# An encoder block in split float32 on one core: both seeds of the seven-product scheme made late, from copies that ScalarE takes of a chain sum

## The chip, the cores and the metric

The kernel runs on one core of a Trainium2 chip. The metric is the device time of one execution in microseconds (us), lower is better. PE is TensorE, DVE is VectorE, ACT is ScalarE, POOL is GpSimd, SP issues most loads.

## The reference

One layer of a hybrid encoder for 256 rows of width 2048, float32 throughout:

```python
h = rms_norm(x, g_mix); proj = h @ w_in          # q, k, v of three attention branches, and 3 gates
oa, ob, oc = ...                                 # dilated windows; grouped-query; cross-attention to mem
gates = sigmoid(gt).reshape(b, s, 3, 2048)
merged = gates[0]*(oa @ w_br_a) + gates[1]*(ob @ w_br_b) + gates[2]*(oc @ w_br_c)
x = x + merged @ w_o
hf = rms_norm(x, g_ffn) @ w_ffn_in               # 2048 -> 2 x 5632
x = x + (silu(hf[..., :5632]) * hf[..., 5632:]) @ w_ffn_out
```

The change touches what comes from the gates on: the gate and branch products with their merge, the output projection, and the FFN.

## The kernel before

**Split products.** Every float32 factor is kept as a high part and a remainder, and each product of blocks is three matmuls: high by high, high by low, low by high. For a weight block (raw, 128 x 1024) ACT makes the high part (`whi`, L413) and DVE the remainder (`wlo`, L423). The activations (xT, oT, mT, x1T, hT) lie ready in both parts. There are five rotating buffers each for whi and wlo, so whi of a step can't be made before PE has ended the step five places earlier.

**Pairs.** From 310 us on the work is a row of 24 pairs: five for the gates (`merging`, blocks b = 0, 1, 2, the last two with two pairs each, j = 0 and 2), two for the output projection (O and O2, `projecting`), eleven for the FFN's input and six for its output (`feeding`). A pair makes two output blocks of 256 x 512 at once, in four accumulators, the PSUM banks X, Y, W and Q. Some of the contraction is done with seven products where eight are usual, on sums of weight blocks and of activations (`forms`). One double m has the seven steps X, W, P, Y, Q, Z, H, each of six matmuls of 128x512. P and Q need a weight sum or difference that DVE makes first (L537, L539), and so does H (L541). The rest of the contraction is done by whole blocks: d into X and Y, D into W and Q.

**Banks and seeds.** P, Q and H accumulate in bank X on top of X's products, one behind the other, so X holds a chain sum; Z accumulates in bank W. At the end of X's products ACT copies bank X to bank Y (L514) as Y's start. At the end of W's, ACT copies bank W to SBUF as m5 (L517; the profile writes m). At the end of P's, DVE writes m5 − X into bank W (L519), and at the end of Q's, m5 − X into bank Q (L523). These two are the seeds of the last two output blocks. Where a bank is fresh, PE sets it with one dummy matmul first (`wake`).

**Order.** A step list per stage, written by hand, sets the order of the steps: l and r are loads (l also starts the POOL queue's accumulating load of the sum of two blocks), a letter with a number is a step, and a point takes one step of the tail that the pair before has left. The second string of a list is worked off without tails, and the third becomes the tail. `run(..., 4)` readies each step (load, weight sum, whi, wlo) four steps ahead of its matmuls; the instructions of each engine then stand in that program order and run in it. `done` functions empty the banks: `gates` and `merge` (L838, L843, L849), `add` (L883), `hidden` (L924 with the Silu table, L927), `output` (L946). Jobs such as the transposes run beside the steps; a `yield n` in one lets n steps pass.

In `add`, the fourth block's job squares its rows, lets two steps pass, transposes, lets two more pass, and then makes the reciprocal root (`row_scale`, L140 to L157: eleven small DVE operations and two copies to the scales), which the Silu of the first FFN pair needs.

Of the kernel before, what the change touches and what calls it, by code (L numbers as in the profile page):

```python
# [11 lines left out]
F32 = mybir.dt.float32  # L12
# [38 lines left out]

STEPS_GATE = ("l0 l1 X0 . X1 . . r0 W0 r1 W1 P0 P1 . Y0 Y1 . Q0 Q1 .", "Z0 Z1 D4 H0 D5 H1 d4 D6 d5 D7 d6 d7", "")
STEPS_O = ("l0 X0 . . r0 . W0 . P0 . Y0 . Q0", "Z0 D2 H0 D3 d2 D6 D7 D4 D5", "d3 d6 d7 d4 d5")
STEPS_O2 = ("l0 X0 . r0 W0 . P0 . Y0 . Q0 .", "Z0 D2 H0 D3 d2 D4 D5 d3 D6 D7", "d4 d5 d6 d7")
STEPS_FFN0 = ("l0 l1 X0 X1 . r0 W0 . r1 W1 . P0 P1 . Y0 Y1 Q0 Q1", "Z0 Z1 D6 H0 D7 H1 D4 D5", "d6 d7 d4 d5")
STEPS_FFN = ("l0 l1 X0 X1 . r0 W0 r1 W1 P0 P1 . Y0 Y1 . Q0 Q1 .", "Z0 Z1 D4 H0 D5 H1 D6 D7", "d4 d5 d6 d7")
STEPS_OUT = STEPS_OUT2 = STEPS_FFN
STEPS_LAST = ("l0 l1 X0 X1 . r0 W0 . r1 W1 . P0 P1 . Y0 Y1 Q0 Q1", "Z0 Z1 H0 H1 D4 D5", "d4 d5")  # L60
# [41 lines left out]
def encoder_block(ctx: ExitStack, tc: tile.TileContext, a: dict, out: bass.AP):  # L102
# [17 lines left out]
    def s4(shape, name, dt=F32):  # L120
        return mid.tile(shape, dt, name=name, tag="s4")
# [300 lines left out]
        while len(due) > n:  # L422
            nc.follow(nc.vector.tensor_sub(*due.pop(0)))  # L423

    def pair(src, lhs, lists, done, doubles=(), forms=None, operand=None, fresh=False):

# [71 lines left out]

        def wake(b, hi):

            if fresh:
                nc.tensor.matmul(ps[b], lhsT=hi[:, 0, :P], rhs=hi[:, 0], start=True, stop=True)

        def phase_end(kind, hi):
            seen[kind] = seen.get(kind, 0) + 1
            if seen[kind] < nd:
                return
            with tc.high_priority():  # L510
                if kind == "X":
                    new("Y")
                    wake("Y", hi)
                    nc.follow(nc.scalar.activation(ps["Y"], ps["X"], AF.Copy))  # L514
                elif kind == "W":
                    raws["m5"] = s4([P, NC], "m5")
                    nc.follow(nc.scalar.activation(raws["m5"], ps["W"], AF.Copy))  # L517
                elif kind == "P":
                    nc.follow(nc.vector.tensor_sub(ps["W"], raws["m5"], ps["X"]))  # L519
                elif kind == "Q":  # L520
                    new("Q")
                    wake("Q", hi)
                    nc.follow(nc.vector.tensor_sub(ps["Q"], raws["m5"], ps["X"]))  # L523

        def seventh(kind, m):
            of = {"X": "b11", "W": "t", "Y": "b21", "P": "t", "Z": "b22", "Q": "b11", "H": "b21"}[kind]
            bk = {"P": "X", "Q": "X", "H": "X", "Z": "W"}.get(kind, kind)
            needs = {"Y": "X", "P": "X", "Z": "P", "Q": "P", "H": "Q"}

            def ready():  # L530
                r = raws[m]
                raw = r[of]
                if kind in "PQH" and last_kind[0] == {"P": "W", "Q": "X", "H": "Y"}[kind] + str(m):
                    low(0)
                last_kind[0] = kind + str(m)
                if kind == "P":
                    nc.follow(nc.vector.tensor_add(raw, raw, r["b22"]))  # L537
                elif kind == "Q":
                    nc.follow(nc.vector.tensor_sub(raw, r["t"], raw))  # L539
                elif kind == "H":  # L540
                    nc.follow(nc.vector.tensor_add(raw, r["t"], raw))  # L541
                hi, lo = halves(raw)
                for n in {"Q": ["b11"], "Z": ["b22"], "H": ["t", "b21"]}.get(kind, ()):
                    release(r.pop(n))

                def products():
                    assert kind not in needs or seen.get(needs[kind], 0) == nd, (kind, seen)
                    assert kind != "Z" or seen["W"] == nd
# [281 lines left out]
    def merging():  # L830
        for b, (g0, k0, k1) in enumerate(((0, 0, 2), (8, 2, 6), (4, 6, 12))):
            for j in (0, 2) if b else (2,):
                sg = [None, None]

                def gates(c, r, sg=sg):
                    sg[c] = s4([P, T, NC], "sg")
                    for t in range(T):
                        nc.scalar.activation(sg[c][:, t], r[t], AF.Sigmoid, scale=r_x[:, 0, t:t + 1])  # L838

                def merge(c, r, j=j, b=b, sg=sg):  # L840
                    n0 = (j + c) * NC
                    for t in range(T):
                        nc.vector.tensor_mul(sg[c][:, t] if b else mg[t][:, n0:n0 + NC], r[t], sg[c][:, t])  # L843

                    def later():
                        yield 1
                        for t in range(T):
                            m = mg[t][:, n0:n0 + NC]
                            nc.vector.tensor_add(m, m, sg[c][:, t])  # L849
                        if b == 2:  # L850
                            to = mT[j + c] = s8([P, 2, 4, S], "mT", pool=home(j + c))
                            if j + c == 0:
                                room.extend(form_room(1))
                            yield 3
                            yield from transposed([mg[t][:, n0:n0 + NC] for t in range(T)],
                                                  lambda k, n: (to[:, 0, k:k + n], to[:, 1, k:k + n]),
                                                  lag=2, also=room[0] if j + c == 0 else None)
                    if b:
                        start(urgent(later()))

                yield pair(block_pair(a["w_gate"], g0 + j), xT, STEPS_GATE, gates, TWO, by_room(lambda: gforms),
                           fresh=b == 0)
# [6 lines left out]
    def projecting():  # L869
# [9 lines left out]
        for n in (0, 2):  # L879
            def add(c, r, n=n):  # L880
# [6 lines left out]
                def later():  # L887
                    yield 1
                    sq = s4([P, T, NC], "sq")
                    for t in range(T):  # L890
                        nc.scalar.activation(sq[:, t], xc[t], AF.Square, accum_out=ss1[:, t, n + c:n + c + 1])
                    yield 2
                    if not x1T:
                        x1T.extend(s8([P, 2, 4, S], "x1T") for _ in range(4))
                        room.extend(form_room(3))
                    yield from transposed(xc, lambda k, m: (x1T[n + c][:, 0, k], x1T[n + c][:, 1, k]),
                                          lambda k: gT[:, 2, 4 * (n + c) + k:4 * (n + c) + k + 1], 2,
                                          also=room[2 + n + c] if n == 0 else None)
# [13 lines left out]
    def feeding():  # L912
        for c0, c1 in ((0, 4), (4, 8), (8, KF // 4)):
# [3 lines left out]
            for n in range(c0, c1):  # L917
                av = []

                def hidden(c, v, av=av, n=n - c0, hT=hT):  # L920
# [8 lines left out]
                    def later():  # L929
# [115 lines left out]
```

## Time and profile before

| | us |
|---|---|
| median of 3 runs (lowest, highest) | 1374.86 (1374.70, 1375.64) |
| the profiled execution's own time | 1373.56 |
| its span | 1371.8 |
| PE busy | 1355.9 (99%) |
| DVE busy | 1154.8 (84%) |
| ACT busy | 852.1 (62%) |

The granted clock of TensorE is 0.999 over the span. The stages: up to 310 us the projections and attention, gates to 600 (with the O pair's start), output projection to about 690, FFN to the end. PE's busy share says little here, since its rows overlap; how far it stands still is read from the gaps between a matmul and the next, and from what released the next. In rows of the timeline, start, duration, engine, line, operation and out<-in are followed by the idle time before, with its releaser, in square brackets. The profile leaves out buffer numbers, so mmX is bank X of any pair and raw any weight block.

### The profile page before, as it was taken

Reading aid. Unit: us, or ns where it says so; the run is one execution under the profiler, and the core shown is the slowest. Engines: PE = TensorE matmul, PEld = TensorE weight load, DVE = VectorE, ACT = ScalarE, POOL = GpSimd, SP = SyncE. Lnnn points to the kernel's source line nnn. Section 1 sums busy time; section 2 is a strip of 40 time slices with the busy share of each in tenths; the row PEclk is TensorE's granted clock in tenths of the full one; section 3 lists DMA queues with packets and bytes.
Section 4 is the critical chain, followed back from the end, with each engine's and each line's share of the span. In section 5 each row is a group of like instructions: output and inputs, shape, how many; then the busy total and the mean of one; then the engine's idle time right before and its main releaser. Section 6 shows DMA issues by size and latency. Waiting matters only on the chain.

```text
span 1371.8 us, 17290 instructions
## 1 busy us (share of the span) xinstructions
PE 1355.9 (99%) x6170; PEld 1121.2 (82%) x6170; DVE 1154.8 (84%) x1411; ACT 852.1 (62%) x1101; POOL 53.2 (4%) x60
## 2 busy tenths in 40 slices
PE   9999999999999999999999999999999999999998
PEld 8878888887787878788878888888888888888887
DVE  6878877779779779778888998888999889989997
ACT  7776666656555555657666666655666655566664
POOL 0010000000000000000000000000000000000000
PEclk9999999999999999999999999999999999999999
DMA  9976455566595595865577666786666786666873
GB/s 368 344 233 212 140 153 182 155 176 223 173 313 172 184 307 156 290 229 166 172 245 227 189 227 203 250 264 215 212 217 218 250 269 191 221 224 214 278 211 108
DMA packets 86342, 301.18 MB, mean 220 GB/s; under 512 B 9776, under 2 KB 12336, under 8 KB 86000
## 3 DMA queue, kind: packets, MB, share of 16 engines
q1 hardware_dynamic: 79488, 275.94, 57.8%
q0 software_dynamic: 6624, 24.12, 9.3%
q8 instruction: 48, 0.79, 0.2%
q14 instruction: 38, 0.31, 0.1%
q10 hardware_dynamic: 144, 0.02, 0.0%
HBM read 297.17 MB, written 2.88 MB: 219 GB/s over the span
## 4 chain that ended last, share of the span: by engine, by line
PE 93%; DVE 5%; issue 1%; ACT 1%; POOL 0%; DVEq 0%; ACTq 0%; POOLq 0%
PE mmX L77 28%; PE mmW L77 19%; PE mm L77 16%; PE mmY L77 14%; PE mmQ L77 11%; DVE wlo L423 3%; PE tp L77 1%; PE sc L77 1%; PE o L77 1%; PE pT L77 1%; DVE raw L539 1%; PE hT L77 0%; DVE sg L843 0%; ACT whi L413 0%; PE idle L77 0%
## 5 line engine op out<-in xcount | busy, mean ns | idle before, releaser
L413 ACT ACTIVATE whi<-raw 128x1024 fp32r<-128x1024 f32 (+1 forms) x359 | 372.2, 1054 | 227.8 <-PE mmQ L77 49.4
L423 DVE TENSOR_TENSOR wlo<-raw,whi 128x1024 fp32r<-128x1024 f32 (+1 forms) x359 | 432.4, 1217 | 94.5 <-ACT whi L413 91.4
L77 PE MATMUL mm<-whi,xT 128*128 128x512 f32 x640 | 202.8, 393 | 0.1
L413 ACT ACTIVATE whi<-more 128x1024 fp32r<-128x1024 f32 x102 | 107.7, 1056 | 68.1 <-DVE more L539 17.5
L131 DVE TENSOR_TENSOR wlo<-raw,whi 128x1024 fp32r<-128x1024 f32 x82 | 103.0, 1258 | 44.8 <-ACT whi L130 43.8
L423 DVE TENSOR_TENSOR wlo<-more,whi 128x1024 fp32r<-128x1024 f32 x102 | 124.2, 1220 | 18.8 <-ACT whi L413 17.8
L77 PEld LDWEIGHTS mm<-whi,xT 128*128 128x128 f32 x640 | 119.5, 188 | 24.2 <-DVE V L134 0.5
L413 ACT ACTIVATE whi<-both 128x1024 fp32r<-128x1024 f32 x92 | 97.2, 1057 | 66.0 <-issue 12.1
L130 ACT ACTIVATE whi<-raw 128x1024 fp32r<-128x1024 f32 x82 | 86.8, 1060 | 66.7 <-PE mm L77 52.1
L423 DVE TENSOR_TENSOR wlo<-both,whi 128x1024 fp32r<-128x1024 f32 x92 | 112.0, 1221 | 19.3 <-ACT whi L413 18.5
L77 PE MATMUL mmW<-whi,forms 128*128 128x512 f32 x368 | 123.2, 394 | 4.1 <-ACT av L924 3.3
L77 PE MATMUL mm<-wlo,xT 128*128 128x512 f32 x320 | 125.8, 393 | 0.0
L77 PE MATMUL mmX<-whi,forms 128*128 128x512 f32 x368 | 122.0, 391 | 2.3 <-DVE mmW L519 2.3
L77 PE MATMUL mmX<-whi,x1T 128*128 128x512 f32 x352 | 120.9, 389 | 0.0
L77 PE MATMUL mmY<-whi,x1T 128*128 128x512 f32 x264 | 88.9, 389 | 0.0
L77 PEld LDWEIGHTS mmW<-whi,forms 128*128 128x128 f32 x368 | 69.7, 190 | 19.8 <-ACT av L924 3.7
L77 PEld LDWEIGHTS mmX<-whi,forms 128*128 128x128 f32 x368 | 69.1, 188 | 17.3 <-ACT whi L413 3.1
L77 PEld LDWEIGHTS mmX<-whi,x1T 128*128 128x128 f32 x352 | 66.1, 188 | 13.7
L77 PE MATMUL mmW<-wlo,forms 128*128 128x512 f32 x184 | 72.3, 393 | 0.0
L77 PE MATMUL mmX<-wlo,forms 128*128 128x512 f32 x184 | 71.7, 390 | 0.0
L77 PEld LDWEIGHTS mm<-wlo,xT 128*128 128x128 f32 x320 | 60.2, 188 | 12.2 <-issue 0.7
L77 PE MATMUL mmX<-wlo,x1T 128*128 128x512 f32 x176 | 68.5, 389 | 0.0
(269 smaller groups left out, 2588.9 us busy)
## 6 DMA issues: line engine op xcount, KB each, us to landing
raw<-in_w_ffn SPq DMA_DIRECT2D x110, 512.0 KB, 6.5
raw<-in_w_gate SPq DMA_DIRECT2D x68, 512.0 KB, 4.7
raw<-in_w_qkv SPq DMA_DIRECT2D x64, 512.0 KB, 4.2
raw<-in_w_ffn_out SPq DMA_DIRECT2D x55, 512.0 KB, 6.8
more<-in_w_ffn SPq DMA_DIRECT2D x33, 512.0 KB, 7.5
both<-in_w_ffn SPq DMA_DIRECT2D x33, 512.0 KB, 5.8
raw<-in_w_o SPq DMA_DIRECT2D x22, 512.0 KB, 5.8
more<-in_w_ffn_out SPq DMA_DIRECT2D x20, 512.0 KB, 5.0
```

The costliest lines, as they stand in the source:

```text
L77: ins = op(*args, **kw)
L130: nc.scalar.activation(hi, src, AF.Copy)
L131: nc.vector.tensor_sub(lo, src, hi.bitcast(F32))
L413: nc.follow(nc.scalar.activation(hi[:, o], v, AF.Copy))
L423: nc.follow(nc.vector.tensor_sub(*due.pop(0)))
L539: nc.follow(nc.vector.tensor_sub(raw, r["t"], raw))
```

## The change

The m5 copy goes. At the end of P's products, and again at the end of Q's, ACT copies the chain sum in bank X to SBUF (u, L520 after). When Q's has been copied, DVE makes both seeds from bank W and these copies: Q = W − u of Q, then W = W − u of P (L525, two rows). Thus Z needs Q's end and not P's, and H needs no more than the copy. The step lists are rewritten for this, those of the gates one per stage: H goes ahead of Z and D, and in some lists Y1 stands behind Q1. `fresh` now names the banks that get the dummy matmul: Y and Q for block 0, Y for the first pair of block 1 (before: Y and Q for block 0). One call per tag shifts the banks by one place ahead of the gates. In `add`, `row_scale` moves ahead of the transposes, one step behind the squares.

```diff
-STEPS_GATE = ("l0 l1 X0 . X1 . . r0 W0 r1 W1 P0 P1 . Y0 Y1 . Q0 Q1 .", "Z0 Z1 D4 H0 D5 H1 d4 D6 d5 D7 d6 d7", "")
+STEPS_GATE = {
+    0: ("l0 l1 X0 X1 r0 W0 r1 W1 P0 P1 Y0 Q0 Q1 Y1 H0 H1", "Z0 D4 Z1 D5 d4 D6 d5 D7 d6 d7", ""),
+    1: ("l0 l1 X0 . X1 r0 W0 r1 W1 P0 P1 . Y0 Q0 Q1 Y1 H0 H1", "Z0 D4 Z1 D5 d4 D6 d5 D7 d6 d7", ""),
+    2: ("l0 l1 X0 . . X1 r0 W0 r1 W1 P0 P1 . Y0 Y1 Q0 Q1 . H0 H1", "Z0 D4 Z1 D5 d4 D6 d5 D7 d6 d7", ""),
+    3: ("l0 l1 X0 . . . X1 r0 W0 r1 W1 . P0 P1 . Y0 Y1 Q0 Q1 . H0 H1", "Z0 D4 Z1 D5 d4 D6 d5 D7 d6 d7", "")}
-STEPS_O = ("l0 X0 . . r0 . W0 . P0 . Y0 . Q0", "Z0 D2 H0 D3 d2 D6 D7 D4 D5", "d3 d6 d7 d4 d5")
+STEPS_O = (". . . l0 X0 . r0 W0 . P0 . Q0 Y0", "H0 d2 Z0 D2 D3 D6 D7 D4 D5", "d3 d6 d7 d4 d5")
-STEPS_FFN0 = ("l0 l1 X0 X1 . r0 W0 . r1 W1 . P0 P1 . Y0 Y1 Q0 Q1", "Z0 Z1 D6 H0 D7 H1 D4 D5", "d6 d7 d4 d5")
-STEPS_FFN = ("l0 l1 X0 X1 . r0 W0 r1 W1 P0 P1 . Y0 Y1 . Q0 Q1 .", "Z0 Z1 D4 H0 D5 H1 D6 D7", "d4 d5 d6 d7")
+STEPS_FFN0 = ("l0 l1 X0 X1 . r0 W0 . r1 W1 . P0 P1 . Y0 Q0 Q1 Y1 H0 H1", "Z0 D6 Z1 D7 D4 D5", "d6 d7 d4 d5")
+STEPS_FFN = ("l0 l1 X0 X1 . r0 W0 r1 W1 P0 P1 . Y0 Y1 Q0 Q1 . H0 H1 .", "Z0 D4 Z1 D5 D6 D7", "d4 d5 d6 d7")
-STEPS_LAST2 = ("l0 l1 X0 X1 . r0 W0 r1 W1 P0 P1 . Y0 Y1 Q0 Q1", "Z0 Z1 D4 H0 D5 H1 d4 d5", "")
+STEPS_LAST2 = ("l0 l1 X0 X1 . r0 W0 r1 W1 P0 P1 . Y0 Q0 Q1 Y1 H0 H1", "Z0 D4 Z1 D5 d4 d5", "")
...
-                elif kind == "W":
-                    raws["m5"] = s4([P, NC], "m5")
-                    nc.follow(nc.scalar.activation(raws["m5"], ps["W"], AF.Copy))
-                elif kind == "P":
-                    nc.follow(nc.vector.tensor_sub(ps["W"], raws["m5"], ps["X"]))
-                elif kind == "Q":
+                elif kind in "PQ":
+                    raws[kind] = s4([P, NC], "u")
+                    nc.follow(nc.scalar.activation(raws[kind], ps["X"], AF.Copy))
+                if kind == "Q":
                     new("Q")
                     wake("Q", hi)
-                    nc.follow(nc.vector.tensor_sub(ps["Q"], raws["m5"], ps["X"]))
+                    for to, u in (("Q", "Q"), ("W", "P")):
+                        nc.follow(nc.vector.tensor_sub(ps[to], ps["W"], raws[u]))
...
-            needs = {"Y": "X", "P": "X", "Z": "P", "Q": "P", "H": "Q"}
+            needs = {"Y": "X", "P": "X", "Z": "Q", "Q": "P", "H": "Q"}
...
+    for tag in ("tp", "c1"):
+        bank("first", tag)
...
-                yield pair(block_pair(a["w_gate"], g0 + j), xT, STEPS_GATE, gates, TWO, by_room(lambda: gforms),
-                           fresh=b == 0)
+                yield pair(block_pair(a["w_gate"], g0 + j), xT, STEPS_GATE[b + (j // 2 if b else 0)], gates, TWO, by_room(lambda: gforms),
+                           fresh=("YQ", "Y" if j == 0 else "", "")[b])
...
+                    if last:
+                        yield 1
+                        ssr = small.tile([P, T], F32, name="ss", bufs=1)
+                        nc.vector.tensor_reduce(ssr, ss1, axis=AX.X, op=ALU.add)
+                        row_scale(ssr, r_f)
                     yield 2
...
-                    if last:
-                        yield 2
-                        ssr = small.tile([P, T], F32, name="ss", bufs=1)
-                        nc.vector.tensor_reduce(ssr, ss1, axis=AX.X, op=ALU.add)
-                        row_scale(ssr, r_f)
...
-            pairs = (STEPS_LAST, STEPS_LAST2) if last else (STEPS_OUT, STEPS_OUT2)
+            pairs = (STEPS_LAST, STEPS_LAST2) if last else (STEPS_FFN, STEPS_FFN)
```

O2's and the first of the last two pairs' lists change in the same manner. Lines after the change are numbered three higher from L77 on and a little more further down: whi is L416, wlo L426, Q's weight differences L541, H's L543.

How the instructions stand, at three places. First gate pair 1 (block 0), the rows of ACT from Y0's copy on before the change: Y0, Y1, m5, Q0, Q1, then Z0, Z1 and D4, and only then H0.

```order
L413 ACTIVATE whi<-raw_3346 128x1024
L413 ACTIVATE whi<-more_3354 128x1024
L517 ACTIVATE m_3407<-mmW 128x512
L413 ACTIVATE whi<-raw_3329 128x1024
L413 ACTIVATE whi<-raw_3334 128x1024
L413 ACTIVATE whi<-raw_3344 128x1024
L413 ACTIVATE whi<-raw_3352 128x1024
L413 ACTIVATE whi<-more_3452 128x1024
L413 ACTIVATE whi<-raw_3346 128x1024
```

The same stretch of ACT after: Y0, Q0, Q1, Y1, u of P, H0, H1, Z0, u of Q, D4.

```order
L416 ACTIVATE whi<-raw_3348 128x1024
L416 ACTIVATE whi<-raw_3331 128x1024
L416 ACTIVATE whi<-raw_3336 128x1024
L416 ACTIVATE whi<-more_3356 128x1024
L520 ACTIVATE u<-mmX 128x512
L416 ACTIVATE whi<-raw_3348 128x1024
L416 ACTIVATE whi<-more_3356 128x1024
L416 ACTIVATE whi<-raw_3346 128x1024
L520 ACTIVATE u<-mmX 128x512
L416 ACTIVATE whi<-more_3471 128x1024
```

H0 has moved up by three places, H1 directly behind it, and the copy that both seeds need stands behind them and Z0. DVE in the same pair before, from Y0's wlo to the seed of Q (L539 makes Q's weights, L541 H's):

```order
L423 TENSOR_TENSOR wlo<-raw_3346,whi 128x1024
L539 TENSOR_TENSOR raw_3329<-raw_3327,raw_3329 128x1024
L423 TENSOR_TENSOR wlo<-more_3354,whi 128x1024
L539 TENSOR_TENSOR raw_3334<-raw_3332,raw_3334 128x1024
L423 TENSOR_TENSOR wlo<-raw_3329,whi 128x1024
L519 TENSOR_TENSOR mmW<-m_3407,mmX 128x512
L423 TENSOR_TENSOR wlo<-raw_3334,whi 128x1024
L423 TENSOR_TENSOR wlo<-raw_3344,whi 128x1024
L423 TENSOR_TENSOR wlo<-raw_3352,whi 128x1024
L541 TENSOR_TENSOR raw_3346<-raw_3327,raw_3346 128x1024
L423 TENSOR_TENSOR wlo<-more_3452,whi 128x1024
L523 TENSOR_TENSOR mmQ<-m_3407,mmX 128x512
```

DVE after, from the row behind P1's wlo to both seeds (L541 makes Q's weights, L543 H's):

```order
L541 TENSOR_TENSOR raw_3331<-raw_3329,raw_3331 128x1024
L426 TENSOR_TENSOR wlo<-raw_3348,whi 128x1024
L541 TENSOR_TENSOR raw_3336<-raw_3334,raw_3336 128x1024
L426 TENSOR_TENSOR wlo<-raw_3331,whi 128x1024
L426 TENSOR_TENSOR wlo<-raw_3336,whi 128x1024
L543 TENSOR_TENSOR raw_3348<-raw_3329,raw_3348 128x1024
L426 TENSOR_TENSOR wlo<-more_3356,whi 128x1024
L543 TENSOR_TENSOR more_3356<-raw_3334,more_3356 128x1024
L426 TENSOR_TENSOR wlo<-raw_3348,whi 128x1024
L426 TENSOR_TENSOR wlo<-more_3356,whi 128x1024
L525 TENSOR_TENSOR mmQ<-mmW,u 128x512
L525 TENSOR_TENSOR mmW<-mmW,u 128x512
```

H's two additions have moved ahead of Y1's wlo and of Z's, and both seeds stand together behind H1's wlo.

Second, ACT at the second FFN pair before: whi of a tail step, of W0, W1, P0, the start of Y, whi of P1 and of a tail step, then the load of the Silu table and the Silu itself (av).

```order
L413 ACTIVATE whi<-raw_6442 128x1024
L413 ACTIVATE whi<-raw_6407 128x1024
L413 ACTIVATE whi<-raw_6411 128x1024
L413 ACTIVATE whi<-raw_6407 128x1024
L514 ACTIVATE mmY<-mmX 128x512
L413 ACTIVATE whi<-raw_6411 128x1024
L413 ACTIVATE whi<-raw_6527 128x1024
L924 ACT_TABLE_LOAD
L924 ACTIVATE av<-mmW,scales 128x512
L924 ACTIVATE av<-mmQ,scales 128x512
```

After, with the same names of steps:

```order
L416 ACTIVATE whi<-raw_6462 128x1024
L416 ACTIVATE whi<-raw_6427 128x1024
L928 ACT_TABLE_LOAD
L928 ACTIVATE av<-mmW,scales 128x512
L928 ACTIVATE av<-mmQ,scales 128x512
L416 ACTIVATE whi<-raw_6432 128x1024
L416 ACTIVATE whi<-raw_6427 128x1024
L517 ACTIVATE mmY<-mmX 128x512
L416 ACTIVATE whi<-raw_6432 128x1024
```

The table load and the Silu stand directly behind W0's whi, ahead of five instructions that stood before them; they follow the scales, whose last row on DVE is now ahead of W0's wlo.

Third, DVE in the last pair before, from Y0's wlo to H's first addition (L946 adds the pair before into x):

```order
L423 TENSOR_TENSOR wlo<-raw_11430,whi 128x1024
L539 TENSOR_TENSOR raw_11383<-raw_11381,raw_11383 128x1024
L423 TENSOR_TENSOR wlo<-more_11452,whi 128x1024
L519 TENSOR_TENSOR mmW<-m_11518,mmX 128x512
L539 TENSOR_TENSOR more_11387<-both,more_11387 128x1024
L946 SCALAR_TENSOR_TENSOR x_5534<-mmY,scales,x_5534 128x512
L423 TENSOR_TENSOR wlo<-raw_11383,whi 128x1024
L946 SCALAR_TENSOR_TENSOR x_5554<-mmX,scales,x_5554 128x512
L423 TENSOR_TENSOR wlo<-more_11387,whi 128x1024
L423 TENSOR_TENSOR wlo<-raw_11428,whi 128x1024
L423 TENSOR_TENSOR wlo<-raw_11450,whi 128x1024
L541 TENSOR_TENSOR raw_11430<-raw_11381,raw_11430 128x1024
```

After, from the row behind the tail step's wlo to H's second addition (L950 adds into x):

```order
L541 TENSOR_TENSOR raw_11434<-raw_11432,raw_11434 128x1024
L426 TENSOR_TENSOR wlo<-more_11482,whi 128x1024
L541 TENSOR_TENSOR raw_11439<-raw_11437,raw_11439 128x1024
L426 TENSOR_TENSOR wlo<-raw_11434,whi 128x1024
L950 SCALAR_TENSOR_TENSOR x_5550<-mmY,scales,x_5550 128x512
L950 SCALAR_TENSOR_TENSOR x_5570<-mmX,scales,x_5570 128x512
L426 TENSOR_TENSOR wlo<-raw_11439,whi 128x1024
L543 TENSOR_TENSOR more_11482<-raw_11432,more_11482 128x1024
L426 TENSOR_TENSOR wlo<-both,whi 128x1024
L543 TENSOR_TENSOR both<-raw_11437,both 128x1024
```

H's additions have moved ahead of Z's remainders, and both of the old seed's subtractions have left this stretch.

More of the change, by code (lines that the diff above doesn't have):

```diff
@@ L48 @@
 MEM_SLOTS = [("kc", _i) for _i in range(4)] + [("vc", _i) for _i in range(4)]
-STEPS_GATE = ("l0 l1 X0 . X1 . . r0 W0 r1 W1 P0 P1 . Y0 Y1 . Q0 Q1 .", "Z0 Z1 D4 H0 D5 H1 d4 D6 d5 D7 d6 d7", "")
-STEPS_O = ("l0 X0 . . r0 . W0 . P0 . Y0 . Q0", "Z0 D2 H0 D3 d2 D6 D7 D4 D5", "d3 d6 d7 d4 d5")
-STEPS_O2 = ("l0 X0 . r0 W0 . P0 . Y0 . Q0 .", "Z0 D2 H0 D3 d2 D4 D5 d3 D6 D7", "d4 d5 d6 d7")
-STEPS_FFN0 = ("l0 l1 X0 X1 . r0 W0 . r1 W1 . P0 P1 . Y0 Y1 Q0 Q1", "Z0 Z1 D6 H0 D7 H1 D4 D5", "d6 d7 d4 d5")
-STEPS_FFN = ("l0 l1 X0 X1 . r0 W0 r1 W1 P0 P1 . Y0 Y1 . Q0 Q1 .", "Z0 Z1 D4 H0 D5 H1 D6 D7", "d4 d5 d6 d7")
-STEPS_OUT = STEPS_OUT2 = STEPS_FFN
-STEPS_LAST = ("l0 l1 X0 X1 . r0 W0 . r1 W1 . P0 P1 . Y0 Y1 Q0 Q1", "Z0 Z1 H0 H1 D4 D5", "d4 d5")
-STEPS_LAST2 = ("l0 l1 X0 X1 . r0 W0 r1 W1 P0 P1 . Y0 Y1 Q0 Q1", "Z0 Z1 D4 H0 D5 H1 d4 d5", "")
+STEPS_GATE = {
[4 rows of a table added]
+STEPS_O = (". . . l0 X0 . r0 W0 . P0 . Q0 Y0", "H0 d2 Z0 D2 D3 D6 D7 D4 D5", "d3 d6 d7 d4 d5")
+STEPS_O2 = ("l0 X0 . r0 W0 . P0 . Q0 . Y0 .", "H0 Z0 D2 D3 d2 D4 D5 d3 D6 D7", "d4 d5 d6 d7")
+STEPS_FFN0 = ("l0 l1 X0 X1 . r0 W0 . r1 W1 . P0 P1 . Y0 Q0 Q1 Y1 H0 H1", "Z0 D6 Z1 D7 D4 D5", "d6 d7 d4 d5")
+STEPS_FFN = ("l0 l1 X0 X1 . r0 W0 r1 W1 P0 P1 . Y0 Y1 Q0 Q1 . H0 H1 .", "Z0 D4 Z1 D5 D6 D7", "d4 d5 d6 d7")
+STEPS_LAST = ("l0 l1 X0 X1 . r0 W0 . r1 W1 . P0 P1 . Y0 Q0 Q1 Y1 H0 H1", "Z0 Z1 D4 D5", "d4 d5")
+STEPS_LAST2 = ("l0 l1 X0 X1 . r0 W0 r1 W1 P0 P1 . Y0 Q0 Q1 Y1 H0 H1", "Z0 D4 Z1 D5 d4 d5", "")
 class InOrder:
@@ L423, in low, with pair @@
             nc.follow(nc.vector.tensor_sub(*due.pop(0)))
-    def pair(src, lhs, lists, done, doubles=(), forms=None, operand=None, fresh=False):
+    def pair(src, lhs, lists, done, doubles=(), forms=None, operand=None, fresh=""):
         lists = [l.split() for l in lists]
@@ L501, in wake @@
         def wake(b, hi):
-            if fresh:
+            if b in fresh:
                 nc.tensor.matmul(ps[b], lhsT=hi[:, 0, :P], rhs=hi[:, 0], start=True, stop=True)
@@ L547, in products @@
                     assert kind not in needs or seen.get(needs[kind], 0) == nd, (kind, seen)
-                    assert kind != "Z" or seen["W"] == nd
+                    assert kind != "Q" or seen["W"] == nd
                     for i in range(2):
```

## The prediction

> **What bounds the kernel now.** I read the page first: the span, the share of each engine, and the chain that ended last.
>
> ```profile
> span 1371.8 us, 17290 instructions
> PE 1355.9 (99%) x6170; PEld 1121.2 (82%) x6170; DVE 1154.8 (84%) x1411; ACT 852.1 (62%) x1101; POOL 53.2 (4%) x60
> PE 93%; DVE 5%; issue 1%; ACT 1%; POOL 0%; DVEq 0%; ACTq 0%; POOLq 0%
> ```
>
> TensorE is the bound, and the change leaves its work alone but for one short matmul. So only its stalls can move the time. The view of waits on PE names them (idle us in total, times, longest), and the busy time by stage tells where the slack is.
>
> ```profile
> PE mmW L77 <- ACT av L924: 3.3, 1, 3.3
> PE mmX L77 <- DVE mmW L519: 2.3, 2, 1.2
> PE mmX L77 <- DVE mg L806: 1.6, 1, 1.6
> ...
> PE mmW L77 <- DVE wlo L423: 1.2, 2, 0.6
> PE mmW L77 <- DVE sg L843: 0.9, 2, 0.4
> PE tp L77 <- DVE mg L849: 0.6, 1, 0.6
> PE mmX L77 <- DVE mmQ L523: 0.5, 1, 0.5
> ```
>
> ```profile
> 740.00:1310.00 570.00, 570.00 (x2554) 471.83 (x2553) 513.31 (x490) 358.02 (x387) 23.39 (x27) 1.00 0.71 229
> ```
>
> The second column is PE's busy time. The FFN stretch from 740 to 1310 has no stall at all: nothing can be won in its 14 steady pairs, only lost. All stalls within reach (10.4 us less the 1.6 behind L806, which after the change still heads the same X0 product) lie in the five gate pairs, the O pair, the second FFN pair and the first of the last two pairs. The view counts idle time only; from start to start each is about 0.15 longer:
>
> ```profile
> 325.69 0.62 PE L77 MATMUL mmY<-whi,xT 128*128 128x512 f32 x2
> ...
> 326.37 0.39 PE L77 MATMUL mmY<-whi,xT 128*128 128x512 f32 x1
> 327.94 0.47 PE L77 MATMUL mmX<-whi,forms 128*128 128x512 f32 x1 [1.19 <-DVE mmW L519]
> ```
>
> Three matmuls in 0.68 us make a pitch of 0.227; six, one product step, take 1.36. Y1 of gate pair 1 ends at 326.60, Q0 starts at 327.94: 1.34 lost.
>
> **What the parts cost.** Durations:
>
> ```profile
> L413 ACT ACTIVATE whi<-raw 128x1024 fp32r<-128x1024 f32 (+1 forms) x359 | 372.2, 1054 | 227.8 <-PE mmQ L77 49.4
> L517 ACT ACTIVATE m<-mmW x24: 574/598/601, 322.2 to 1340.4; 128x512 f32<-128x512 f32 x24
> L519 DVE TENSOR_TENSOR mmW<-m,mmX x24: 685/694/697, 327.1 to 1343.9; 128x512 f32<-128x512 f32 x24
> L541 DVE TENSOR_TENSOR raw<-raw,raw x22: 1212/1218/1220, 331.1 to 1351.5; 128x1024 f32<-128x1024 f32 x22
> ```
>
> Per pair ScalarE (ACT) gets one copy more, 24 × 0.6 = 14 us on an engine busy 62%: of itself nothing, since it is not the bound. The two DVE subtractions stay two. No load is added. The l entries, with POOL's accumulating loads, stay at the head of each list but the O list's, where three tail steps go ahead of them; SP's loads follow the readying of steps. No stall above is put down to a transfer, so I cost them at nothing; if that cover went, a late load would show as a wait of whi on a transfer. What counts is the place in the queues. P's copy stands on ACT in front of Q0's use of bank X; Q's copy stands behind the whi copies of the next four steps, which wait for DVE's adds for H; behind it wait H0 (which overwrites bank X), both DVE subtractions, and with them Z and D4.
>
> **Gate pair 1, in full.** DVE has no idle there but one gap of 0.24:
>
> ```profile
> 315.14 1.22 DVE L537 TENSOR_TENSOR raw<-raw,raw 128x1024 f32<-128x1024 f32 x1
> 318.67 2.52 DVE L423 TENSOR_TENSOR wlo<-raw,whi 128x1024 fp32r<-128x1024 f32 x2
> 321.42 1.23 DVE L423 TENSOR_TENSOR wlo<-raw,whi 128x1024 fp32r<-128x1024 f32 x1 [0.24 <-ACT whi L413]
> 322.56 1.22 DVE L539 TENSOR_TENSOR raw<-raw,raw 128x1024 f32<-128x1024 f32 x1
> ```
>
> Up to P1's wlo (ends 321.2) its order is unchanged. Then, in the rows of the order shown above, come Q's two adds, Y0, Q0, Q1, H's first add, Y1, H's second add: eight at a pitch of 1.14, from 321.1 on. The last ends at 321.1 + 7 × 1.14 + 1.22 = 330.3. ACT then copies H1, Z0 and u, three in a row:
>
> ```profile
> 316.47 1.06 ACT L413 ACTIVATE whi<-raw 128x1024 fp32r<-128x1024 f32 x1 [2.76 <-DVE raw L537]
> ...
> 326.17 2.96 ACT L413 ACTIVATE whi<-raw 128x1024 fp32r<-128x1024 f32 x3 [1.23 <-DVE raw L539]
> ```
>
> Three whi copies take 2.96, so 0.95 each in a row. A copy starts 0.11 after its add (the add of 315.14 ends at 316.36, the copy starts at 316.47). So u ends at 330.3 + 0.11 + 2 × 0.95 + 0.6 = 332.9, and H0 starts near 333.0. Without waits it would start at 326.60 + 2 × 1.36 (Q0 Q1 moved in front, Y1 behind) + 0.23 (wake) = 329.5. So 3.5 are lost, partly already at Q0, where P's copy stands behind whi of Q1 (about 327.4). Now 1.34 is lost: **+2.2**.
>
> **The last pair**, by the same working:
>
> ```profile
> 1340.46 1.22 DVE L423 TENSOR_TENSOR wlo<-raw,whi 128x1024 fp32r<-128x1024 f32 x1
> 1347.40 0.74 DVE L946 SCALAR_TENSOR_TENSOR x<-mmX,scales,x 128x512 f32<-128x512 f32 x1
> 1351.12 0.39 PE L77 MATMUL mmW<-whi,forms 128*128 128x512 f32 x1
> ```
>
> From 1340.46 on DVE carries eight operations of 1.14 and two additions to x of 0.66 before H's second add ends: 1340.46 + 8 × 1.14 + 2 × 0.66 = 1350.9. Copies: + 0.11 + 1.9 + 0.6 = 1353.5. The sixth product after P ends at 1351.12 (today Z0 starts there without idle), so H0 loses about 2.5 where nothing is lost now: **+2.5**.
>
> **The other places**, worked likewise. Gate pair 2 (list 1): second H add ends 377.3, u 380.0, H0 free at 377.5: 2.6 against 1.27 now, **+1.4**. Pairs 3 and 4 (list 2): Z0 now waits for both subtractions and its own wlo, all on a DVE without gaps; 2.1 against 0.9 now, **+1.2 each**. Pair 5 (list 3): W0's 0.6 goes (it comes later), but the transposes wait longer, since the last gate addition stands behind three more wlo; 3.0 against 1.3, **+1.6**. O pair: its W0 wait goes, **−0.6**.
>
> **Second FFN pair.** Its 3.3 us is the largest wait:
>
> ```profile
> 708.02 1.22 DVE L423 TENSOR_TENSOR wlo<-raw,whi 128x1024 fp32r<-128x1024 f32 x1
> 715.91 1.28 ACT L924 ACT_TABLE_LOAD   x1
> 717.07 0.16 DVE L156 COPY scales<-rs_y 128x2 f32<-128x2 f32 x1
> 717.26 0.69 ACT L924 ACTIVATE av<-mmW,scales 128x512 f32<-128x512 f32 x1
> 718.00 0.80 PE L77 MATMUL mmW<-whi,forms 128*128 128x512 f32 x1 [3.25 <-ACT av L924]
> 315.37:318.00 2.63, 2.63 (x12) 2.16 (x13) 2.60 (x3) 1.06 (x1) 0.00 (x0) 1.00 0.32 128
> 718.00:720.60 2.60, 2.60 (x6) 2.12 (x7) 0.00 (x0) 0.53 (x1) 0.00 (x0) 0.50 0.57 202
> ```
>
> av waits for the scales, and the table load before it ends at 717.19 too: moving the scales alone would win 0.1. But the order moves the load and av up as well, right behind W0's first whi. DVE makes the scales ahead of W0's wlo, which today runs at 708.02; with 1.28 for the load and two times 0.69, av is done by about 710.7, and W0, due at 714.6, waits for nothing. That wins 3.4 and the slow start behind it: six matmuls in 2.53 instead of 1.36, at a granted clock of 0.50. Together −4.6. Against it, in the first FFN pair u stands behind squares, transposed copies and H1's whi, and H0 waits about 1.9. **−2.7**.
>
> The row of 718.00 is the only stall after which the clock fell; behind the 1.6 us stall at 315.37 it stayed at 1.00. The Trainium skill ("TensorE: Matmul & The Clock Gate", Part 1) says that the clock halves after an idle window of about 3.4 us: the trace agrees with that at these two stalls, and by it my new stalls, 3.0 at most (pair 1's 3.5 is split in two), cost only themselves. The nearest row, 3.25, would charge the stalls of pair 5 and the last pair 1.17 more each, 2.3 in all. I take none, and keep 2.3 for the range.
>
> **First of the last two pairs:** u is ready near 1321.7, H0 free near 1320.1: 1.6 against 0.7, **+0.9**.
>
> **Steady FFN pairs.** The first stretch of this kind:
>
> ```profile
> 763.97 1.23 DVE L423 TENSOR_TENSOR wlo<-more,whi 128x1024 fp32r<-128x1024 f32 x1
> ...
> 777.58 0.39 PE L77 MATMUL mmY<-whi,x1T 128*128 128x512 f32 x1
> ```
>
> The first row is Y0's wlo. Behind it DVE has Q's add, Y1, Q's second add (ends 763.97 + 3 × 1.14 + 1.22 = 768.6), then Q1's wlo once its whi is copied (769.9), H's add, a tail's wlo and H's second add: 769.9 + 3 × 1.14 + 1.22 = 774.5. ACT: H1, the tail, u: + 0.11 + 2 × 0.95 + 0.6 = 777.1. H0 would start at 777.58, the second row, and needs u about 0.15 before: a margin of 0.3. I add nothing, but little is left.
>
> Sum: 2.2 + 1.4 + 2.4 + 1.6 − 0.6 − 2.7 + 0.9 + 2.5 = +7.7 us. The profiled execution took 1373.56 (1371.8 of span and 1.8 around it); that gives 1381.3 there. The median of the runs stands 1.3 higher, so I forecast 1382.6.
>
> **Rivals.** *Faster: Q's copy is hidden.* DVE no longer stands at P's end waiting for its last product, so it could run ahead. If H's second add ended 3.5 us earlier in pair 1 (by 326.8) and 2.5 earlier in the last pair, H0 would wait nowhere, and the stalls go: 1.34 + 1.27 + 2 × 0.78 + 1.3 + 0.6 + 4.6 + 0.7 − 0.23 = 11.1, to 1364. For it: those DVE waits at P's end are real. Against it: DVE's rows in the gate pair leave no gap to win. Chance 0.18, with a part of the gain (to 1372) likelier than all.
>
> *Much slower: the steady pairs stall.* The margin is 0.3; with 0.3 to 0.6 lost in each of 14 pairs, 4 to 8 us come on top, with the clock's 2.3 at the worst: 1387 to 1393. For it: every pair has the same queue; against it: a margin is left, and DVE has idle there (513 of 570 busy). Chance 0.17.
>
> *No difference:* gate pairs lose half of what I count, and the gain of 4.6 pays for it: 1372 to 1378. Chance 0.14.
>
> *The banks' shift does nothing:* the added pair of bank calls moves addresses, but X0 of pair 1 still follows the same multiplication; the 1.6 of L806 stays. I count on it at 0.9; otherwise 1.7 less, inside the range.
>
> My own forecast (1379 to 1387) holds 0.51. About 0.2%, 2.7 us, is what a measurement of this kernel can tell. Slower is 0.51 + 0.17, same 0.14, faster 0.18. The range 1371 to 1391 leaves out most of the full gain and the worst end.
>
> **What would show it.** Waits on PE headed by ACT's u (L520) at H0 in pairs 1, 2 and the last, of 1.5 to 3 us; Z0 waiting for L525 or wlo in pairs 3 and 4; no wait for av and a granted clock of 1.00 near 718; 740 to 1310 still at 100% for PE. I am wrong if the view of waits names u nowhere, or names it 14 times in the steady stretch.

## The result: 0.8% slower, and where it stands in the profile after

The changed kernel takes 1386.15 us (median of 4 runs, 1385.30 to 1386.62) against 1375.02 for the kernel before on the same chip (4 runs, 1374.70 to 1375.64): 11.1 us more, a ratio of 1.008, 95% interval 1.0062 to 1.0097. I had forecast 7.7 more. The profiled execution took 1385.68, its span is 12.1 longer than that of before.

The page of the changed kernel: span, shares, and the chain that ended last. PE has one more matmul and the same work; the chain could be followed back over only about half of the span here, so the waits are read from the next view.

```profile
span 1383.9 us, 17390 instructions
PE 1359.6 (98%) x6171; PEld 1120.5 (81%) x6171; DVE 1157.2 (84%) x1411; ACT 866.2 (63%) x1125; POOL 53.1 (4%) x60
PE 48%; DMA 0%; DVE 0%; ACT 0%; issue 0%; SPq 0%; DVEq 0%
```

The waits on PE after (idle us in total, times, longest):

```profile
PE mmX L80 <- ACT u L520: 12.7, 8, 2.4
PE tp L80 <- DVE mg L853: 2.8, 1, 2.8
PE mmX L80 <- DVE mg L808: 1.6, 1, 1.6
...
PE mmW L80 <- DVE wlo L426: 1.3, 3, 0.6
PE mmW L80 <- DVE sg L847: 0.2, 1, 0.2
```

Gone are the wait for av, both waits for the seed of W, the wait for Q's seed and most of those for sg. In their place PE waits for ACT's copy u eight times, 12.7 us in all. As before, no wait on PE is put down to a transfer. The wait behind the gate multiplication (L808, X0 of pair 1) is the same 1.6. To see how places add up I summed, from the start of each matmul to the start of the next, what is above the pitch (0.227 us for 128x512), by stretches between the same pairs:

| lost start to start, us | before | after | change | forecast |
|---|---|---|---|---|
| gate and O pairs | 9.4 | 17.3 | +7.9 | +7.0 |
| second output projection pair | 0.5 | 1.8 | +1.3 | 0 |
| first two FFN pairs | 4.95 | 2.0 | −2.95 | −2.7 |
| steady FFN pairs | 1.7 | 3.2 | +1.5 | 0 |
| first of the last two | 0.95 | 0.35 | −0.6 | +0.9 |
| last pair | 0 | 4.5 | +4.5 | +2.5 |
| sum | 17.5 | 29.15 | +11.65 | +7.7 |

Gate pair 1 shows how the wait arises. One row of DVE, three of ACT and two of PE after, from their timelines:

```profile
329.41 1.23 DVE L543 TENSOR_TENSOR more<-raw,more 128x1024 f32<-128x1024 f32 x1
```

```profile
330.75 1.06 ACT L416 ACTIVATE whi<-more 128x1024 fp32r<-128x1024 f32 x1 [1.35 <-DVE more L543]
331.71 1.04 ACT L416 ACTIVATE whi<-raw 128x1024 fp32r<-128x1024 f32 x1
332.66 0.58 ACT L520 ACTIVATE u<-mmX 128x512 f32<-128x512 f32 x1
```

```profile
327.33 0.50 PE L80 MATMUL mmX<-whi,forms 128*128 128x512 f32 x1 [1.85 <-ACT u L520]
...
333.29 0.49 PE L80 MATMUL mmX<-whi,xT 128*128 128x512 f32 x1 [1.36 <-ACT u L520]
```

H's second addition ends at 330.64, ACT copies H1 and Z0, then u, which ends at 333.24, and H0 starts at 333.29. Bank X had been complete since Q1's end at 330.2: u was ready to run for 2.5 us and stood in its queue.

### The profile page after: what moved, and what is told of

Same layout as the page of the kernel before. It is cut to its first block, busy times and chain, and to the rows that moved or that the text cites. A ratio compares the mean times of both kernels' runs of the same rounds, so it can differ in the third digit from the quotient of the medians.

```text
span 1383.9 us, 17390 instructions
## 1 busy us (share of the span) xinstructions
PE 1359.6 (98%) x6171; PEld 1120.5 (81%) x6171; DVE 1157.2 (84%) x1411; ACT 866.2 (63%) x1125; POOL 53.1 (4%) x60
## 5 line engine op out<-in xcount | busy, mean ns | idle before, releaser
L416 ACT ACTIVATE whi<-raw 128x1024 fp32r<-128x1024 f32 (+1 forms) x381 | 398.1, 1056 | 258.3 <-PE mmQ L80 89.7
L426 DVE TENSOR_TENSOR wlo<-raw,whi 128x1024 fp32r<-128x1024 f32 (+1 forms) x381 | 461.5, 1219 | 106.2 <-ACT whi L416 102.4
L80 PE MATMUL mmW<-whi,forms 128*128 128x512 f32 x368 | 126.0, 392 | 0.2 <-DVE sg L847 0.2
L416 ACT ACTIVATE whi<-more 128x1024 fp32r<-128x1024 f32 x87 | 91.3, 1056 | 54.7 <-DVE more L543 14.7
L416 ACT ACTIVATE whi<-both 128x1024 fp32r<-128x1024 f32 x85 | 89.6, 1057 | 53.6 <-PE mmQ L80 16.2
L426 DVE TENSOR_TENSOR wlo<-more,whi 128x1024 fp32r<-128x1024 f32 x87 | 105.8, 1221 | 16.5 <-ACT whi L416 14.3
L426 DVE TENSOR_TENSOR wlo<-both,whi 128x1024 fp32r<-128x1024 f32 x85 | 103.1, 1221 | 18.0 <-ACT whi L416 17.3
L80 PEld LDWEIGHTS mmX<-whi,x1T 128*128 128x128 f32 x352 | 66.1, 188 | 17.8 <-ACT u L520 4.2
```

The source lines that it names most:

```text
L80: ins = op(*args, **kw)
L416: nc.follow(nc.scalar.activation(hi[:, o], v, AF.Copy))
```

## Experiments

Each kernel ran in three rounds beside the kernel before, whose median in the three groups was 1374.51, 1374.76 and 1374.68.

**1 and 2: the root's place.** Experiment 1 makes this edit alone in the kernel before, experiment 2 takes it back in the changed kernel.

```diff
+                    if last:
+                        yield 1
...
-                    if last:
-                        yield 2
```

> The kernel before with one part of the change: the reciprocal root one step behind the squares instead of behind the transposes. Theory A (my prediction's remark that moving the scales alone wins 0.1): the instruction order shows the scales still behind the same tail step's wlo and the table load still behind P1's whi, so the stall of 3.3 us at the second FFN pair stays, with the half clock behind it: 1375.0, within 0.7. Rival B (the move of the root is what removes the stall): 4.6 us less, 1370.4, and no wait for av.

> The changed kernel with the root put back behind the transposes. Theory A (the new step lists, not the root's place, moved the scales and the Silu ahead): the scales stand two DVE rows later, about 2.4 us, and the Silu is still done before W0 needs its bank: 1386.2, within 1 us, no wait for av. Rival B: the stall and the half clock return, 1390.7.

Experiment 1: 1373.76 (ratio 0.9994, 0.9985 to 1.0004). The wait stays:

```profile
PE mmW L77 <- ACT av L924: 3.9, 1, 3.9
```

Experiment 2: 1386.61 (1384.84 to 1386.95), as the changed kernel, and no wait for av. So the move of the root, done or undone, is worth nothing in time here. By place it isn't nothing in the changed kernel. With it undone, the 1.7 lost at H0 of the first FFN pair is gone, and PE waits for u six times, 9.8 us, instead of eight times. ACT's first copy of the transposes there waits 0.17 us for PE instead of 1.53, which fits the edit's `yield 1`: it puts these transposes one step later. In the profiled execution a half clock behind the stalls of gate pairs 1 and 2 took most of the gain back (18.7 lost in the gate and O pairs instead of 17.3).

The stall at av is gone in both kernels, since in both the scales' rows stand ahead of W1's wlo on DVE, and the Silu ahead of P0's whi on ACT. In the changed kernel the Silu ends at 721.75, and W0 starts at 726.07. The new lists bring this order, but they aren't needed for it: experiment 5 has it with the old lists and the new seeds (744.38 and 748.70), and experiment 7 in the kernel before.

**3: the new lists with the old seeds.** m5 and its two subtractions come back, the lists stay.

```diff
-                elif kind in "PQ":
-                    raws[kind] = s4([P, NC], "u")
-                    nc.follow(nc.scalar.activation(raws[kind], ps["X"], AF.Copy))
+                elif kind == "W":
+                    raws["m5"] = s4([P, NC], "m5")
+                    nc.follow(nc.scalar.activation(raws["m5"], ps["W"], AF.Copy))
+                elif kind == "P":
+                    nc.follow(nc.vector.tensor_sub(ps["W"], raws["m5"], ps["X"]))
...
```

> The changed kernel with the seeds made as before (m5 from W on ACT, m5 - X on DVE at P's and at Q's end), in the new step lists. Theory A (the cost is that H follows Q directly, so that whatever has to read bank X between them is on the path, be it ACT's copy or DVE's subtraction): H0 waits for the subtraction on DVE instead of for u, which stands behind H's additions and wlo: 1384 to 1389, with the waits on PE now at H0 for L523's twin. Rival B (the extra copy on ACT and both seeds made late are the cost): back near the kernel before, 1375 to 1379.

1405.11 (ratio 1.0227, 1.0211 to 1.0242): neither. It is 19 us slower than the changed kernel, and 15.6 us are lost in the steady stretch against 3.2. Its waits on PE:

```profile
PE mmX L80 <- ACT whi L416: 18.3, 18, 3.0
PE mmX L80 <- DVE mmQ L526: 5.6, 4, 1.9
```

H0 waits for its own whi, since H's additions are late on DVE; the old seed of W stands among them:

```profile
778.50 1.22 DVE L426 TENSOR_TENSOR wlo<-raw,whi 128x1024 fp32r<-128x1024 f32 x1
779.64 0.69 DVE L522 TENSOR_TENSOR mmW<-m,mmX 128x512 f32<-128x512 f32 x1
780.23 1.22 DVE L542 TENSOR_TENSOR raw<-raw,raw 128x1024 f32<-128x1024 f32 x1
```

DVE has no idle left there, so 0.6 us more ahead of H is more than the margin of 0.3 that I had worked out for this stretch. With these lists the new seeds are the better ones.

**4: both copies u earlier in ACT's order.** A step marked soon has its matmuls, and with them the copy, issued up to two steps ahead; the seeds keep their place.

```diff
-                    new("Q")
-                    wake("Q", hi)
-                    for to, u in (("Q", "Q"), ("W", "P")):
-                        nc.follow(nc.vector.tensor_sub(ps[to], ps["W"], raws[u]))
+                    owed.append((popped[0] + 4, lambda: seeds(hi)))
...
+                products.soon = kind in 'PQ'
...
+                while getattr(waiting[0], "soon", False) and len(waiting) > ahead - 2:
+                    emit(waiting.pop(0))
```

> The changed kernel with the two copies u issued up to two steps earlier in ACT's order, ahead of the whi copies of the two steps that are readied last (H1 and Z0 for Q's copy, Q1 and Y1 for P's); DVE's order and PE's order are unchanged. Theory A (u waits for its place in ACT's queue behind whi copies that wait for DVE): the 12.7 us of waits for u fall below 4; DVE then limits gate pairs 1 to 4 (H's wlo, the seeds), so not all is won: 1377 to 1381. Rival B (DVE's H additions set the end anyway, ACT's queue is cover): the waits move to wlo, 1384.5 to 1386.5.

1402.46 (ratio 1.0209, 1.0193 to 1.0224): 16 us slower than the changed kernel, and outside both forecasts. No wait for u is left. As rival B says, the waits moved to wlo, but they grew; 21 waits of Y's products and others are new:

```profile
PE mmW L80 <- DVE wlo L427: 9.2, 9, 1.8
PE mmY L80 <- DVE wlo L427: 6.7, 21, 0.4
PE mmX L80 <- DVE wlo L427: 3.9, 6, 0.8
```

The steady stretch loses 15.2. ACT and DVE there:

```profile
776.75 0.60 ACT L528 ACTIVATE u<-mmX 128x512 f32<-128x512 f32 x1 [2.66 <-PE mmX L80]
```

```profile
778.33 1.23 DVE L427 TENSOR_TENSOR wlo<-raw,whi 128x1024 fp32r<-128x1024 f32 x1 [1.47 <-ACT whi L416]
```

P's copy, now ahead of the whi of Y1, holds ACT for 2.66 us until P's last product, and DVE then idles 1.47 for a whi. The copy either waits in the queue or makes the queue wait. The Trainium skill ("TensorE: Matmul & The Clock Gate", Part 1) calls ACT's and DVE's queues strictly first in, first out; this row agrees.

**5: the new seeds in the old lists.**

> The changed kernel with all step lists as before the change, and the new seeds (two copies u, both subtractions behind Q's). Theory A (the lists put H directly behind Q and make the loss; the seeds cost only where Z follows Q directly): Z0 there waits for u, both subtractions and its wlo, about 2.3 us in the five gate pairs (which lose 5.5 of stalls they have now), and in the O, the first FFN and the last two pairs; steady pairs have a tail step between and lose nothing: 1383 to 1391, with Z0 at the head of the waits and H0 nowhere. Rival B (the lists are all of the loss, the seeds none): 1374 to 1377.

```diff
-    0: ("l0 l1 X0 X1 r0 W0 r1 W1 P0 P1 Y0 Q0 Q1 Y1 H0 H1", "Z0 D4 Z1 D5 d4 D6 d5 D7 d6 d7", ""),
...
+G = ("l0 l1 X0 . X1 . . r0 W0 r1 W1 P0 P1 . Y0 Y1 . Q0 Q1 .", "Z0 Z1 D4 H0 D5 H1 d4 D6 d5 D7 d6 d7", "")
+STEPS_GATE = {k: G for k in range(4)}
...
```

1414.61 (ratio 1.0291, 1.0276 to 1.0306): the place was right and the size too small, 4.5 to 5.3 us in each of the first four gate pairs instead of 2.3. Behind five of its stalls the clock halved as well, which cost 10.8 us more.

```profile
PE mmW L78 <- DVE mmW L523: 28.5, 7, 5.1
```

ACT at gate pair 3 in this kernel:

```profile
445.75 1.06 ACT L414 ACTIVATE whi<-raw 128x1024 fp32r<-128x1024 f32 x1 [3.70 <-DVE raw L541]
446.71 0.58 ACT L518 ACTIVATE u<-mmX 128x512 f32<-128x512 f32 x1
```

In the old list H0 is the fourth step behind Q1, so u stands behind H0's whi, and that waits 3.70 us for H's addition: the same queue again, in another list. The steady pairs lose 2.8 against 1.7 before. Each half of the change alone, the lists in experiment 3 and the seeds here, is worse than both together.

**6: Q's copy alone earlier.** Against experiment 4:

```diff
-                products.soon = kind in 'PQ'
+                products.soon = kind in 'Q'
```

> The changed kernel with Q's copy u alone issued two steps earlier in ACT's order (P's copy stays). Theory A (an early P copy held ACT at P's end and so made whi, and then wlo, late in the steady pairs, 15.2 us from 740 to 1310 instead of 3.2; Q's early copy holds nothing, since H1's addition comes later anyway): the steady stretch loses 2 us or less, the waits for u shrink to those for P's copy (2.0 in gate pair 1, 1.3 in the second output projection pair), DVE limits the gate pairs: 1379 to 1384. Rival B (any copy ahead of whi holds ACT): steady pairs lose about 1 us each as with both: 1395 to 1402.

1386.80 (1383.24 to 1388.20): no gain over the changed kernel, against my 1379 to 1384; rival B's 1395 to 1402 fell as well. By place the expectation was half right. The steady stretch is back to 1.8 lost and the last pair to 2.2 from 4.5, but the gate and O pairs lose 19.8 instead of 17.3, 2.3 of it by a slow clock behind a stall of 4.2:

```profile
PE mmW L80 <- DVE wlo L427: 6.6, 8, 1.8
PE tp L80 <- DVE mg L868: 4.2, 1, 4.2
PE mmX L80 <- ACT u L528: 3.0, 2, 1.8
```

There the wait moved from u to DVE: Z0's wlo, and the last gate addition in pair 5. This fits ACT's queue being one of two limits that lie close together in the gate pairs; no run here relieved DVE without making the sums slower.

**8: the change in the gate pairs alone.** Their lists, seeds and dummy matmuls; the rest as before.

```diff
+                elif late:
+                    if kind in "PQ":
...
-            needs = {"Y": "X", "P": "X", "Z": "Q", "Q": "P", "H": "Q"}
+            needs = {"Y": "X", "P": "X", "Z": "Q" if late else "P", "Q": "P", "H": "Q"}
```

> The change in the five gate pairs alone (their lists, seeds, dummy matmuls and the banks' shift); the output projection and the FFN as before. Theory A (the loss is the sum of separate places, as the gaps of the trace add up): the stretch 312 to 600 loses 17.3 instead of 9.4 and the rest is as before: 1374.8 + 7.9 = 1382.7, 1381 to 1385 with or without a slow clock behind a stall. Rival B (places act on one another: later pairs give time back or lose more): outside that.

1384.44 (1383.57 to 1386.89, ratio 1.0076). The stretch lost 19.4 in the profiled execution, of which 1.6 is a slow clock behind one stall; without it 17.8 against 17.3 in the changed kernel, and the other stretches are those of before, with the 3.3 for av. The places add up.

**9 and 10: weight sums on POOL.** H's additions in the changed kernel (9), Q's differences in the kernel of experiment 7 below (10), in the gate pairs.

```diff
+                by = nc.gpsimd if kind in pooled else nc.vector
...
-                    nc.follow(nc.vector.tensor_add(raw, r["t"], raw))
+                    nc.follow(by.tensor_add(raw, r["t"], raw))
```

> The changed kernel with the weight sums for H0 and H1 of the gate pairs made by POOL instead of DVE. Theory A (in the gate pairs DVE's queue sets the end; ten additions of 1.14 leave it): if POOL's addition takes 2.5 us or less, the loss from 312 to 600 falls from 17.3 by 4 to 8: 1378 to 1382. Rival B (ACT's order sets it: u stays behind H1's whi, which waits for a sum that POOL makes more slowly): no gain or a loss, 1386 or more. The duration of POOL's addition is shown by no run so far.

> The kernel before with the root in one piece, and the weight differences for Q0 and Q1 of the gate pairs made by POOL instead of DVE. Theory A (DVE's queue makes Q0 wait for the seed of W in pairs 1 and 2, 2.6 us in all, and D4's wlo late in pairs 3 and 4, 1.6): without two operations of 1.14 ahead of it the seed is made when P ends: 1365 to 1368. Rival B (POOL is slower than the slack): whi of Q0 is late instead, 1369.3 or more.

1398.57 and 1379.12 (ratios 1.0173 and 1.0035): rival B in both; experiment 10 is 9.9 above experiment 7, on which it is built. The groups of POOL's additions in 9 and of its subtractions in 10:

```profile
L544 POOL TENSOR_TENSOR raw<-raw,raw 128x1024 f32<-128x1024 f32 x5 | 20.0, 4006 | 87.4 <-DVE wlo L426 87.4
```

```profile
L540 POOL TENSOR_TENSOR raw<-raw,raw 128x1024 f32<-128x1024 f32 x7 | 22.6, 3230 | 90.8 <-DVE raw L538 76.6 <-DMA both<-in_w_gate 12.9 <-issue 1.3
```

In these groups POOL takes 3.2 to 4.0 us (one addition of experiment 9 took 6.7) for what DVE does in 1.22. A POOL product of the same size had taken 2.40 in the kernel before, a row that the expectation of experiment 9 overlooked. In 9 the waits for u rise to 15.0, as they must if u stands behind a whi that waits for H's sum. That DVE's load limits the gate pairs is thereby not shown, since POOL's own delay covers it.

**7: the kernel before with the root in one piece.** Its fifteen small rows are chained in DVE's order at their old place.

```diff
-                        nc.vector.tensor_reduce(ssr, ss1, axis=AX.X, op=ALU.add)
-                        row_scale(ssr, r_f)
+                        nc.follow(nc.vector.tensor_reduce(ssr, ss1, axis=AX.X, op=ALU.add))
+                        row_scale(ssr, r_f, nc.follow)
```

> The kernel before with one edit: the eleven small operations of the root, its sum and the two copies are kept together in DVE's order, at their old place behind the transposes, instead of being spread between wlo operations. By the order the table load and the Silu then stand behind W0's whi, as in the changed kernel. Theory A (the stall at the second FFN pair is a matter of where the scales stand in DVE's order): the wait of 3.3 us and the half clock behind it go, DVE is held for about 2.5 us near 696, where no wait is seen: 4.6 less than before, 1370 to 1371.5. Rival B (held together, the root makes a wlo late near 696): 1372 to 1375.

1369.27 (5 runs, 1368.96 to 1369.71), ratio 0.9960, 0.9946 to 0.9974: the fastest of all, 5.5 us below the kernel before, where I had expected 3.3 to 4.8. The rows of ACT:

```profile
708.76 1.28 ACT L924 ACT_TABLE_LOAD   x1
710.06 0.69 ACT L924 ACTIVATE av<-mmW,scales 128x512 f32<-128x512 f32 x1
```

Against 715.91 and 717.26 before. The stretch of the first two FFN pairs loses 0.8 instead of 4.95, with 0.5 of it at a new wait for a wlo near 703.5. These 4.15 are not all of the 5.5. The rest is probably the clock: the runs of experiment 7 show a granted clock of 0.999 to 1.000, those of the kernel before beside them 0.997 to 0.999.

## Why the prediction was right, step by step

**Direction and mechanism: right; the size was low.** Measured in lost time, the change costs 11.65 instead of 7.7: four places lost 5.7 more than forecast, two lost 1.75 less, and that these partly cancel is luck. The forecast rested on u's place behind whi copies that wait for H's additions. The chain in gate pair 1 came as written: H's second addition ends at 330.64 (330.3 forecast), u at 333.24 (332.9), H0 at 333.29 (333.0); 2.0 lost at Q0 and 1.5 at H0, 3.5 together as forecast.

**Terms that held.** Pair 2: 2.6 at H0 (2.6). Pairs 3 and 4: 2.1 each (2.1), but half of it stands at H0 behind u, where I had put all of it at Z0; that the sum came out is luck. Pair 5: 2.9 at the transposes and 0.3 at W0 (3.0). First FFN pair: 1.7 (1.9). The wait for av and the half clock behind it went, −4.8 (−4.6). Last pair: 2.6 at H0 (2.5).

**The step on the root.** I wrote that the scales' move alone wins 0.1, and that the order moves the Silu up. Experiment 1 bears the first out. That the move itself costs 1.7 at H0 of the first FFN pair, as experiment 2 shows, I hadn't seen: I had counted that wait, but not what made it. Experiment 7 shows that the same gain needs none of the new lists.

**Terms that were mis-sized.**
- The second output projection pair, put at nothing: 1.3. I had looked at H0 only. Q0 waits for P's copy, which stands on ACT behind copies of transposes that wait for DVE. ACT there, after:

```profile
640.93 0.84 ACT L311 ACTIVATE ffull<-tp,gT 128x256 f32<-128x256 f32 x2 [1.05 <-DVE x1T L137]
```

- The steady pairs: margin 0.3 forecast, and five of them wait 0.18 for u; the stretch lost 1.5 more. The margin was right to within half a microsecond, the zero was not. I had read off PE's busy time that nothing was lost there before; from start to start it was 1.7.
- First of the last two pairs: a loss of 0.9 forecast, a gain of 0.6 measured. u ends at 1328.64 and H0 starts at 1328.69: four transposes, 0.56 of PE time that I had left out, stand between Y1 and H0. The rest is u, which came about 1 us earlier than forecast once the 8.0 are taken off by which the kernel ran late there; why wasn't traced.
- The last pair: 1.9 us on top, 1.7 of them a slow clock. I had taken none of it, since no new stall reached the idle window that I had quoted, though the nearest row, a stall of 3.25, priced it at 1.17. That step failed. The granted clock behind two equal stalls of 2.6 us (window, then PE, PEld, DVE, ACT, POOL busy, clock, transfers):

```profile
382.60:385.20 2.60, 2.56 (x11) 2.14 (x12) 2.58 (x4) 2.60 (x3) 0.00 (x0) 1.00 0.85 339
1361.60:1364.90 3.30, 3.30 (x8) 2.62 (x9) 3.30 (x4) 2.17 (x3) 0.00 (x0) 0.50 0.32 129
```

**The rivals.** The faster one fell: DVE did not run ahead in the gate pairs. No difference fell too: the gate and O pairs lost 7.9 more, not half of 7.0. That the steady pairs stall was right for 1.5 of its 4 to 8 us. The banks' shift did nothing to the wait at L808, as counted on.

## What the runs showed of the clock

In the profiled executions of all twelve kernels, 15 stalls of PE were 3.0 us or longer, and behind 14 of them the following matmuls came at about 0.43 us instead of 0.227. Of 20 stalls from 2.0 to 3.0 us, 7 were followed by it. Of 45 from 1.3 to 2.0, 4 were, and these 4 are two cases of two stalls within 3 us of each other. The same stall of 2.0 us at Q0 of gate pair 1 left the clock alone in the changed kernel and halved it in experiment 2 (stall, then what followed):

```profile
324.00:326.80 2.80, 0.94 (x6) 0.43 (x4) 2.73 (x4) 2.49 (x3) 0.00 (x0) 1.00 0.27 26
326.80:329.80 3.00, 3.00 (x8) 2.42 (x9) 2.97 (x3) 1.06 (x1) 0.00 (x0) 0.60 0.86 291
```

So a stall of 2 to 3 us costs itself and, now and then, 1.5 to 1.7 us more; the changed kernel has four of these, and its runs spread over 1.3 us.

The traces also hold the times at which the granted clock changed, and these show what decides. In each of the twelve, every change lies a whole number of slices of 3.413 us after the first change (in the kernel before, the next one comes 208 slices later), and each half clock ahead of the last matmul lasts one or two slices. Where the slices lie against the kernel's start differs from execution to execution. Cut along them from 20 us on, and without the last two, the twelve traces have 4737 slices at full clock. Of the 20 in which PE was busy for less than 1.5 us, all were followed by half clock; of 15 from 1.5 to 1.8, three; of the 4702 above that, none. What counts is how much of a stall falls into one slice. The two stalls of 2.6 us in the changed kernel show it: the first is shared by two slices, the second lies in one (slices one after the other, columns as above).

```profile
378.53:381.94 3.41, 1.68 (x7) 0.86 (x5) 3.31 (x4) 2.07 (x3) 0.00 (x0) 1.00 0.65 252
381.94:385.36 3.42, 2.72 (x12) 2.26 (x13) 3.21 (x5) 3.42 (x5) 0.00 (x0) 1.00 0.88 290
...
1358.15:1361.57 3.42, 1.01 (x5) 0.48 (x3) 3.15 (x4) 2.52 (x4) 0.00 (x0) 1.00 1.00 322
1361.57:1364.98 3.41, 3.39 (x8) 2.71 (x9) 3.41 (x4) 2.28 (x3) 0.00 (x0) 0.50 0.32 129
```

At Q0 of gate pair 1, PE was busy for 1.57 us of its slice in the changed kernel and for 1.54 in experiment 2, where either end occurs. So which stalls of 2 to 3 us halve the clock can't be read from the program alone; it also depends on where the slices lie in that execution.

The Trainium skill ("TensorE: Matmul & The Clock Gate", Part 1) asks for an idle window of about 3.4 us; the measurements say that a stall of 2.0 can be enough. The Trainium skill also says there that the window runs freely, without regard to when work starts; the slices above agree in length and in this.

## What stays open

Whether the gate pairs of the changed kernel could be made as fast as before by relieving DVE wasn't settled: POOL was too slow to try it with. Nor was any run made that moves a stall against the slices of the clock and changes nothing else.

## What to carry to other kernels

A copy that frees a bank costs what stands ahead of it in its engine's queue, not its own 0.6 us; find its row in the program order, then the last thing that the rows ahead of it wait for, and add up from there. Moving such a copy ahead only helps where its input comes before the work that it passes: in the steady pairs it held up everything behind it. And before buying a gain with a rearrangement, look whether one chain of small instructions, kept together, buys it alone: here that was worth 5.5 us, and the rearrangement cost 11.
